# A two-block transformer on one core: expert weights in 16 KB runs, buffers of two units, three modulation steps moved, overflow loads issued by GpSimd

## Chip, cores and metric

One core of a Trainium2 chip runs the whole program in one launch. The metric is the device time of one execution in microseconds, the median of several. All inputs lie in the chip's memory in layouts that the host has prepared; preparing them is not timed. Engines: PE multiplies, PEld loads its weights, DVE, ACT and POOL (GpSimd) do the vector work, SP only issues transfers, and 16 DMA engines carry them.

## What is computed

256 tokens of width 1024, all in f32. Block 1 is attention with 8 heads, a layer norm, a mixture of 32 experts of which each token uses four, and another layer norm. Block 2 is two layers of attention (16 heads) and a gated feed-forward net, each modulated by vectors that come from `c` through `w_mod`.

```
t = moba_attention(h, w_in, w_out, rel_bias)
h = layer_norm(ALPHA * h + t)
top_logit, top_e = top_k(h @ w_router + b_router, 4); gate = softmax(top_logit)
# for each expert e and the tokens that chose it:
a = xs @ w_gu[e] + b_gu[e];  g, u = split(a)           # w_gu[e]: 1024 x 2048
g = min(g, 7);  u = clip(u, -7, 7)
y = (g * sigmoid(1.702 * g) * (u + 1)) @ w_down[e] + b_down[e]   # w_down[e]: 1024 x 1024
h = layer_norm(ALPHA * h + sum over the 4 of gate * y)
for i in range(2):                                      # block 2
    mod = silu(c) @ w_mod[i] + b_mod[i]                 # 1024 x 6144: six shifts, scales, gates
    x = x + gt_a * rmsnorm(attention(modulate(rmsnorm(x), sh_a, sc_a)) @ w_o[i])
    h = modulate(rmsnorm(x), sh_f, sc_f)
    x = x + gt_f * rmsnorm((silu(conv(h @ w_gate)) * (h @ w_up)) @ w_down[i])
```

## The kernel before

**The weight stream.** Every weight matrix comes as a row of 547 units of 1 MB, each a tile of 128 partitions x 2048 f32 and each used once. `Stream` (from L63) holds their order. `pump` (L85) issues the next unit on SP (L100) as soon as one of the open pools has a free buffer; `take` (L111) hands the next unit to the code that uses it, counts the one before as free and pumps. The pools are m (11 buffers, from the start), x (2 more, opened in the attention) and y (5 more, opened when the attention's space is given back, for units up to expert 20, closed at expert 24). A call of `take` fixes only the order; on the chip SP waits, instruction by instruction, until the engine that reads the old content is done. SP's transfers use eight semaphores in turn, so eight are under way at most.

**Order of the units** (`make_stream`, L204): queries, keys and values of attention 1, with four units of `w_mod` between them; four of `w_out`; then for each expert e eight gate-up units and four down units of expert e-1; the last expert's four down units; four units of `w_mod`; the weights of block 2. A gate-up unit is 128 rows of `w_gu[e]`, 8 KB a partition in one run. A down unit is 256 rows of `w_dn[e]`, two runs of 4 KB a partition.

**The expert loop** (`moe`, L798). PE multiplies the 64 token slots of an expert with the units in f32: `gate_up` (L698; bias L706, matmuls L715, eight a unit in the trace, since an f32 matmul shows twice) and `down` (L772, matmuls L783). Between the units it transposes and gathers for the neighbouring experts (L692, L740, L750, L763, L765) and adds the previous expert's rows (L795). In expert 24 comes `overflow` (L908): a branch (L916) on the largest count of tokens of an expert. Its body handles counts over 64, with loads of its own on SP; it is not entered with these inputs, but its branch stands on every engine.

**Modulation.** `fill` (L244) does n modulation steps: one unit of `w_mod`, four matmuls with `c` (L241). Four steps stand in the attention loop (`MOD_A`), four at the start of block 2 (`MOD_PRE`).

**Routing** (`norm1`, from L582): for each half of 128 tokens the residual sums (L597), `bn_stats` (L674), scaling (L599), transposes (L606), logits (L560, copy L622, sum L624), choice (L627 to L635). PE runs warm-up matmuls (L161) in its gaps; `WARM` gives their numbers.

Of the kernel before, what the change touches and what calls it, by code (L numbers as in the profile page):

```python
# [18 lines left out]
P = 128  # L19
# [10 lines left out]
NWB = 11  # L30
NXB = 2
NYB = 5
TOE = 16
OVER = 24
MOD_A = (1,1,1,1,0,0,0,0,0,0)
MOD_A_LAST = max(i for i in range(10) if MOD_A[i])
DVE_MOD = {(0, 1): 0, (1, 0): 0}
WARM = (8, 20, 4, 4, 4)
# [3 lines left out]
MOD_PRE = ((4, 0), (6, 0))  # L42
# [20 lines left out]
class Stream:  # L63
    def __init__(self, nc, srcs):
        self.nc = nc
        self.srcs = srcs
        self.pools = {}
        self.order = []
        self.tiles = {}
        self.where = {}  # L70
        self.issued = 0
        self.taken = 0
        self.limit = {}
        self.after = {}
        self.hold = len(srcs)
# [8 lines left out]

    def pump(self):  # L85
        while self.issued < self.hold:
# [7 lines left out]
            t = self.pools[key][0].tile([P, UNIT], F32, name=f"wu_{key}", tag=f"wu_{key}")  # L94
            src = self.srcs[i]
            if isinstance(src, list):
                for c0, c1, part in src:
                    self.nc.sync.dma_start(t[:, c0:c1], part)
            else:
                self.nc.sync.dma_start(t, src)  # L100
            for f in self.after.pop(i, ()):
                f()
            self.tiles[i] = t
            self.where[i] = key
            self.issued += 1
# [5 lines left out]
    def take(self):  # L111
        i = self.taken
        if i > 0:
            self.pools[self.where[i - 1]][1] += 1
            self.tiles.pop(i - 1)
            self.pump()
        self.taken += 1
        return self.tiles[i]


class Kernel:
# [79 lines left out]
    def make_stream(self):  # L201
# [10 lines left out]
        for i in range(10):  # L212
            u.append(ap["w_qk"][i] if i < 8 else outs[i - 8])
            m(MOD_A[i])
        u.extend(outs[2:])
        gu = lambda e: u.extend(ap["w_gu"][e, k * P:(k + 1) * P, :] for k in range(NK))
        dn = lambda e: u.extend(ap["w_dn"][e, k * 256:(k + 1) * 256, :].rearrange("(j p) n -> p j n", p=P) for k in range(4))
# [6 lines left out]
        dn(NE - 1)  # L224
        self.moe_end = len(u)
        self.stream_l2(u, m)
        self.st = Stream(self.nc, u)

# [15 lines left out]
    def fill(self, n, pool, pause=False):  # L244
# [3 lines left out]
        for i in range(n):  # L248
# [3 lines left out]
            if self.mps is None:  # L252
                self.mps = self.bank("acc", "modps")
# [101 lines left out]
    def attention1(self, a, a2):  # L355
# [44 lines left out]
        self.st.after = {2: [early], 3: [router], 5: [toeplitz_write], 6: [toeplitz_read], 8: [load_x], 10: [later]}  # L400
        self.st.hold = 5
# [92 lines left out]
        for i in range(10):  # L494
# [13 lines left out]
            self.fill(MOD_A[i], a2, i == MOD_A_LAST)()  # L508
# [12 lines left out]
        self.flush_mod()  # L521
        self.pause_mod()()
# [59 lines left out]
    def norm1(self):  # L582
# [12 lines left out]
        def rows(t):  # L595
            for h in range(2):
                nc.vector.scalar_tensor_tensor(x[:, t, hs[h]], x[:, t, hs[h]], ALPHA, self.ybank[h][t], op0=ALU.mult, op1=ALU.add)  # L597
            self.layer_stats([x[:, t, hs[0]], x[:, t, hs[1]]], t, mv, rs)
# [19 lines left out]
        def logits(t):  # L618
# [3 lines left out]
            nc.scalar.copy(part, ps[:, 0:P])  # L622
            lgs[t] = self.bank("acc")
# [18 lines left out]
        self.warm(WARM[4], "sc", self.cst.bitcast(BF16))  # L642
# [4 lines left out]
        self.warm(WARM[2], "sc", self.cst.bitcast(BF16))  # L647
        choose(1)

# [10 lines left out]
        self.warm(WARM[3], "sc", self.cst.bitcast(BF16))  # L660
# [7 lines left out]
        nc.vector.tensor_copy(self.cnt, cm)  # L668

    def layer_stats(self, halves, t, mv, rs):  # L670
        nc = self.nc
        bs = self.mk.tile([P, 2, 6], F32, name="bs", tag=f"bs{t}")
        for h in range(2):
            nc.vector.bn_stats(bs[:, h, :], halves[h])  # L674
# [214 lines left out]
    def norm2(self, banks, lnp):  # L889
# [5 lines left out]
        for t in range(2):  # L895
            self.layer_stats(banks[t], t, mv, rs)
# [10 lines left out]
    def overflow(self, banks):  # L907
# [8 lines left out]
        with tc.If(rv > CAP):  # L916
            with tc.For_i(0, NE, 1) as e:
# [10 lines left out]
                def gu_unit(k):  # L928
                    t = unit()
                    nc.sync.dma_start(t, ap["w_gu"][bass.ds(e, 1), k * P:(k + 1) * P, :].rearrange("o p n -> (o p) n"))  # L930
                    return t

                def dn_unit(k):
                    t = unit()
                    nc.sync.dma_start(t.rearrange("p (j n) -> p j n", j=2),
                                      ap["w_dn"][bass.ds(e, 1), k * 256:(k + 1) * 256, :].rearrange("o (j p) n -> p (o j) n", p=P))
# [547 lines left out]
```

## Time and profile before

| what | value |
|---|---|
| runs | 1736.28, 1736.58, 1737.66 us; median 1736.58 |
| profiled execution, its own time | 1736.98 us |
| its span | 1735.3 us |
| PE busy | 1672.9 us, 96% of the span |
| DVE, ACT, POOL busy | 739.8, 484.4, 82.3 us |
| moved by the DMA engines | 584.92 MB, mean 337 GB/s |
| first and last gate-up or down matmul | 135.84 us and 1072.8 us |

The span runs from the first instruction to the last; the execution's time lies 1.7 us above it. A busy share is an average over attention 1 with the routing (to 136 us), the MoE (to 1073 us) and block 2. PE's share counts a matmul as busy until its modelled end. A DMA share over 1 means that packets of one engine overlap.

### The profile page before, as it was taken

What the parts mean: (1) busy time and instruction counts of PE and PEld (TensorE: products, weight loads), DVE (VectorE), ACT (ScalarE), POOL (GpSimd) and SP (SyncE); (2) the same over time, 40 slices, a digit from 0 to 9 for tenths busy, and PEclk for the clock granted to TensorE, in tenths of its full rate; (3) what the DMA queues carried; (4) which work ended last, traced back from release to release, by engine and by line L of the source; (5) the groups of instructions that cost most, each with busy time, mean ns of one, the idle gap of its engine ahead of it and who ended that gap; (6) DMA issues with size and microseconds to landing.
All of it is one profiled execution on the core that took longest, in us unless ns stands there. A gap on an engine that the chain in (4) does not pass through costs nothing.

```text
span 1735.3 us, 23418 instructions
## 1 busy us (share of the span) xinstructions
PE 1672.9 (96%) x9690; PEld 975.5 (56%) x9690; DVE 739.8 (43%) x1196; ACT 484.4 (28%) x806; POOL 82.3 (5%) x113
## 2 busy tenths in 40 slices
PE   9999999999999999999899998999999999999998
PEld 6873333333333332333233322787999868879997
DVE  4662121221222112121121213896666867766654
ACT  4531000000001000000000001555655356565543
POOL 0000000000000020000000000031000003200000
PEclk9999999999999999999999999999999999999999
DMA  9969999999999999999989999974855986585520
GB/s 304 413 250 383 419 416 417 417 416 417 416 418 416 417 417 417 417 416 418 412 358 418 415 418 416 420 275 159 365 205 171 353 324 193 162 323 200 194 73 25
DMA packets 105655, 584.92 MB, mean 337 GB/s; under 512 B 11856, under 2 KB 13352, under 8 KB 54984
## 3 DMA queue, kind: packets, MB, share of 16 engines
q1 hardware_dynamic: 103736, 577.96, 83.5%
q0 software_dynamic: 1808, 5.41, 1.3%
q8 instruction: 78, 1.28, 0.3%
q14 instruction: 33, 0.27, 0.0%
HBM read 582.05 MB, written 1.28 MB: 336 GB/s over the span
## 4 chain that ended last, share of the span: by engine, by line
PE 36%; DMA 9%; DVE 3%; issue 1%; ACT 1%; POOL 0%; DVEq 0%; POOLq 0%; ACTq 0%; SPq 0%
PE ps_mm L145 6%; PE ps_mm L146 5%; PE ps_mm L147 5%; DMA wu_m<-w_dn 5%; DMA wu_m<-w_gu 3%; PE ps_sc L145 3%; PE ps_sc L146 3%; PE ps_sc L147 3%; PE ps_mm L715 1%; PE modps L241 1%; PE ps_acc L145 1%; DMA wu_x<-w_gu 1%; PE ps_acc L147 1%; PE ps_acc L146 1%; PE ps_tr L783 1%
## 5 line engine op out<-in xcount | busy, mean ns | idle before, releaser
L715 PE MATMUL ps_mm<-wu_m,xg 128*64 128x512 f32 x1400 | 329.1, 602 | 4.8 <-DMA wu_m<-w_gu 4.1
L140 DVE TENSOR_TENSOR wL<-wu_m,wH 128x1024 fp32r<-128x1024 f32 x226 | 267.3, 1225 | 142.5 <-ACT wH L139 142.5
L139 ACT CAST wH<-wu_m 128x1024 fp32r<-128x1024 f32 x226 | 225.9, 1049 | 104.2 <-PE ps_mm L146 66.2
L715 PEld LDWEIGHTS ps_mm<-wu_m,xg 128*64 128x64 f32 x1400 | 92.8, 137 | 198.0 <-issue 168.5
L783 PE MATMUL ps_tr<-wu_m,aT 128*64 128x512 f32 x752 | 174.7, 597 | 18.1 <-DMA wu_m<-w_dn 16.8
L145 PE MATMUL ps_mm<-hH,wH 128*128 128x256 f32 x608 | 174.9, 288 | 0.0
L147 PE MATMUL ps_mm<-hL,wH 128*128 128x256 f32 x608 | 172.0, 283 | 0.2 <-DVE hL L1060 0.2
L146 PE MATMUL ps_mm<-hH,wL 128*128 128x256 f32 x608 | 171.9, 283 | 0.0
L783 PEld LDWEIGHTS ps_tr<-wu_m,aT 128*64 128x64 f32 x752 | 50.6, 136 | 137.2 <-issue 82.6
L145 PEld LDWEIGHTS ps_mm<-hH,wH 128*128 128x128 f32 x608 | 116.4, 191 | 7.8 <-issue 6.5
L147 PEld LDWEIGHTS ps_mm<-hL,wH 128*128 128x128 f32 x608 | 116.5, 192 | 0.4 <-DVE hL L1060 0.4
L146 PEld LDWEIGHTS ps_mm<-hH,wL 128*128 128x128 f32 x608 | 116.5, 192 | 0.0
L787 DVE SCALAR_TENSOR_TENSOR yL<-ps_tr,gs,yH 128x512 fp32r<-128x512 f32 x32 | 24.0, 751 | 214.3 <-ACT yH L786 214.3
L695 ACT COPY gs<-ps_tr 128x512 f32<-128x512 f32 x32 | 18.8, 586 | 339.1 <-PE ps_tr L692 339.1
L769 DVE COPY gs<-ps_tr 128x1 f32<-128x1 f32 x32 | 5.1, 158 | 236.9 <-ACT s L767 236.9
L146 PE MATMUL ps_sc<-hH,wL 128*128 128x256 f32 x352 | 99.7, 283 | 0.0
L145 PE MATMUL ps_sc<-hH,wH 128*128 128x256 f32 x352 | 99.6, 283 | 0.0
L147 PE MATMUL ps_sc<-hL,wH 128*128 128x256 f32 x352 | 99.6, 283 | 0.0
L786 ACT ACTIVATE yH<-ps_tr,gs 128x512 fp32r<-128x512 f32 x32 | 22.0, 687 | 242.8 <-PE ps_tr L783 242.8
L715 PE MATMUL ps_mm<-wu_y,xg 128*64 128x512 f32 x368 | 85.9, 599 | 0.0
L730 ACT ACTIVATE sg<-g 128x512 f32<-128x512 f32 x32 | 20.2, 631 | 212.8 <-DVE g L729 212.8
L742 DVE COPY aT<-ps_tr 128x512 f32<-128x512 f32 x32 | 22.1, 691 | 132.6 <-PE ps_tr L740 132.6
(346 smaller groups left out, 2525.7 us busy)
## 6 DMA issues: line engine op xcount, KB each, us to landing
wu_m<-w_gu SPq DMA_DIRECT2D x175, 1024.0 KB, 19.9
wu_m<-w_dn SPq DMA_DIRECT2D x94, 1024.0 KB, 20.0
wu_m<-w_mod SPq DMA_DIRECT2D x48, 1024.0 KB, 6.7
wu_y<-w_gu SPq DMA_DIRECT2D x46, 1024.0 KB, 19.8
wu_m<-w_fg_u SPq DMA_DIRECT2D x44, 1024.0 KB, 8.2
wu_x<-w_gu SPq DMA_DIRECT2D x35, 1024.0 KB, 19.9
wu_m<-w_qk SPq DMA_DIRECT2D x24, 1024.0 KB, 13.1
wu_m<-w_fd SPq DMA_DIRECT2D x22, 1024.0 KB, 5.0
```

The costliest lines, as they stand in the source:

```text
L139: nc.scalar.copy(h[:, sl], src[:, sl])
L140: nc.vector.tensor_tensor(lo[:, sl], src[:, sl], h[:, sl].bitcast(F32), op=ALU.subtract)
L145: mm(out, lh, rh, start=start, stop=False)
L146: mm(out, ll, rh, start=False, stop=False)
L147: mm(out, lh, rl, start=False, stop=stop)
L695: nc.scalar.copy(gs, g)
L715: mm(ab[i][64 * h:64 * h + 64, :], self.chunk(xg, k), u[:, c:c + 512], start=False, stop=k == NK - 1, tile_position=(0, 64 * h))
L730: nc.scalar.activation(sg, g, AF.Sigmoid, scale=1.702)
L742: nc.vector.tensor_copy(aT, tp)
L783: nc.tensor.matmul(o[64 * h:64 * h + 64, :], lhs, u[:, c:c + 512], start=f == 0, stop=f == NK - 1, tile_position=(0, 64 * h))
L786: nc.scalar.activation(yH, o, AF.Copy, scale=gate)
L787: nc.vector.scalar_tensor_tensor(yL, o, gate, yH.bitcast(F32), op0=ALU.mult, op1=ALU.subtract)
```

## The change

1. **Pairs.** Units are taken in pairs. A buffer is a tile [128, 2, 2048] and comes free when both units are used. The pools are 5, 1 and 3 pairs (18 units as before). Where the next two units are a `Pair`, one transfer of 2 MB loads both; elsewhere two transfers of 1 MB as before.
2. **Layouts.** The host lays `w_gu` and `w_dn` out in pairs, so that a partition's share of a pair is one run of 16 KB. All experts' gate-up units and the down units of experts 0 to 30 are `Pair`s; the last expert's four down units are single transfers with 8 KB runs. `w_fd` of block 2 gets 8 KB runs for 4 KB.
3. **Modulation.** The four steps leave the attention loop; three stand in the routing, where eight warm-up matmuls leave, and at the start of block 2 there are five instead of four, behind 16 warm-up matmuls instead of 20.
4. **`layer_stats`** computes half a row's residual and its statistics in turn, where both residuals came first.
5. **Overflow** loads are issued on GpSimd's queue instead of SP's.
6. At the start the stream holds after six units instead of five, and the bias table's store and load come after units 6 and 7.

```diff
-NWB = 11
-NXB = 2
-NYB = 5
+NWB = 5
+NXB = 1
+NYB = 3
-MOD_A = (1,1,1,1,0,0,0,0,0,0)
-MOD_A_LAST = max(i for i in range(10) if MOD_A[i])
+MOD_A = 3
-WARM = (8, 20, 4, 4, 4)
+WARM = (8, 16, 4)
-MOD_PRE = ((4, 0), (6, 0))
+MOD_PRE = ((5, 0), (6, 0))
...
+    def load(self, t, src):
+        if isinstance(src, list):
+            for c0, c1, part in src:
+                self.nc.sync.dma_start(t[:, c0:c1], part)
+        else:
+            self.nc.sync.dma_start(t, src)
     def pump(self):
         while self.issued < self.hold:
             for key in self.order:
...
                 return
             i = self.issued
             self.pools[key][1] -= 1
-            t = self.pools[key][0].tile([P, UNIT], F32, name=f"wu_{key}", tag=f"wu_{key}")
-            src = self.srcs[i]
-            if isinstance(src, list):
-                for c0, c1, part in src:
-                    self.nc.sync.dma_start(t[:, c0:c1], part)
-            else:
-                self.nc.sync.dma_start(t, src)
-            for f in self.after.pop(i, ()):
-                f()
-            self.tiles[i] = t
+            t = self.pools[key][0].tile([P, 2, UNIT], F32, name=f"wu_{key}", tag=f"wu_{key}")
+            n = min(2, len(self.srcs) - i)
+            if isinstance(self.srcs[i], Pair):
+                self.nc.sync.dma_start(t, self.srcs[i].ap)
+            for j in range(i, i + n):
+                if not isinstance(self.srcs[i], Pair):
+                    self.load(t[:, j - i, :], self.srcs[j])
+                for f in self.after.pop(j, ()):
+                    f()
+                self.tiles[j] = t[:, j - i, :]
             self.where[i] = key
-            self.issued += 1
+            self.issued += n
     def resume(self):
         self.hold = len(self.srcs)
...
     def take(self):
         i = self.taken
         if i > 0:
-            self.pools[self.where[i - 1]][1] += 1
             self.tiles.pop(i - 1)
-            self.pump()
+            if i % 2 == 0:
+                self.pools[self.where[i - 2]][1] += 1
+                self.pump()
         self.taken += 1
         return self.tiles[i]
+class Pair:
+    def __init__(self, ap):
+        self.ap = ap
...
-        for i in range(10):
-            u.append(ap["w_qk"][i] if i < 8 else outs[i - 8])
-            m(MOD_A[i])
-        u.extend(outs[2:])
-        gu = lambda e: u.extend(ap["w_gu"][e, k * P:(k + 1) * P, :] for k in range(NK))
-        dn = lambda e: u.extend(ap["w_dn"][e, k * 256:(k + 1) * 256, :].rearrange("(j p) n -> p j n", p=P) for k in range(4))
+        u.extend(ap["w_qk"][i] for i in range(8))
+        u.extend(outs)
+        m(MOD_A)
+        def pairs(w):
+            for d in range(w.shape[0]):
+                u.extend([Pair(w[d].rearrange("p (j n) -> p j n", j=2)), None])
+        gu = lambda e: pairs(ap["w_gu"][e])
+        dn = lambda e: pairs(ap["w_dn"][e])
         for e in range(NE):
             gu(e)
             if e > 0:
                 dn(e - 1)
             if e == OVER - 4:
                 self.y_end = len(u)
-        dn(NE - 1)
+        u.extend(self.dn_part(ap["w_dn"][NE - 1], k) for k in range(4))
         self.moe_end = len(u)
         self.stream_l2(u, m)
         self.st = Stream(self.nc, u)
+    def dn_part(self, w, k):
+        return w[k // 2, :, (k % 2) * UNIT:(k % 2) * UNIT + UNIT]
...
-        self.st.after = {2: [early], 3: [router], 5: [toeplitz_write], 6: [toeplitz_read], 8: [load_x], 10: [later]}
-        self.st.hold = 5
+        self.st.after = {2: [early], 3: [router], 6: [toeplitz_write], 7: [toeplitz_read], 8: [load_x], 10: [later]}
+        self.st.hold = 6
...
-            self.fill(MOD_A[i], a2, i == MOD_A_LAST)()
...
         def rows(t):
-            for h in range(2):
+            def half(h):
                 nc.vector.scalar_tensor_tensor(x[:, t, hs[h]], x[:, t, hs[h]], ALPHA, self.ybank[h][t], op0=ALU.mult, op1=ALU.add)
-            self.layer_stats([x[:, t, hs[0]], x[:, t, hs[1]]], t, mv, rs)
+                return x[:, t, hs[h]]
+            self.layer_stats(half, t, mv, rs)
...
             nc.scalar.copy(part, ps[:, 0:P])
+            self.fill(1, a2, False, "sc")
             lgs[t] = self.bank("acc")
             mm(lgs[t][:, 0:NE], part, self.eyes, start=True, stop=True)
...
         logits(0)
-        self.warm(WARM[4], "sc", self.cst.bitcast(BF16))
         turn(1)
         turned(1)
         choose(0)
         logits(1)
-        self.warm(WARM[2], "sc", self.cst.bitcast(BF16))
         choose(1)
+        partial = self.fill(MOD_A - 2, a2, True, "sc")
...
+        partial()
...
-            nc.vector.bn_stats(bs[:, h, :], halves[h])
+            nc.vector.bn_stats(bs[:, h, :], half(h))
...
-                    nc.sync.dma_start(t, ap["w_gu"][bass.ds(e, 1), k * P:(k + 1) * P, :].rearrange("o p n -> (o p) n"))
+                    nc.gpsimd.dma_start(t, ap["w_gu"][bass.ds(e, 1), k // 2, :, (k % 2) * UNIT:(k % 2) * UNIT + UNIT].rearrange("o p n -> (o p) n"))
...
-                    nc.sync.dma_start(t.rearrange("p (j n) -> p j n", j=2),
-                                      ap["w_dn"][bass.ds(e, 1), k * 256:(k + 1) * 256, :].rearrange("o (j p) n -> p (o j) n", p=P))
+                    nc.gpsimd.dma_start(t, ap["w_dn"][bass.ds(e, 1), k // 2, :, (k % 2) * UNIT:(k % 2) * UNIT + UNIT].rearrange("o p n -> (o p) n"))
...
-    A["w_gu"] = asc(f("moe_w_gate_up")[0])
+    A["w_gu"] = asc(f("moe_w_gate_up")[0].reshape(NE, 4, 2, P, UNIT).transpose(0, 1, 3, 2, 4).reshape(NE, 4, P, 2 * UNIT))
-    A["w_dn"] = asc(f("moe_w_down")[0])
+    A["w_dn"] = asc(f("moe_w_down")[0].reshape(NE, 2, 4, P, D).transpose(0, 1, 3, 2, 4).reshape(NE, 2, P, 2 * UNIT))
...
-    A["w_fd"] = asc(f("w_ffn_down_2"))
+    A["w_fd"] = asc(f("w_ffn_down_2").reshape(2, NF // 2, 2, P, D).transpose(0, 1, 3, 2, 4).reshape(2, NF // 2, P, UNIT))
```

How the change stands in the programs, first on SP around the overflow branch (a row is the line, the instruction, and its target, source and shape; `x4` is four alike). Before:

```order
L100 DMA wu_m<-w_dn 128x2x1024 x4
L915 TENSOR_LOAD cnt
L916 COMPARE_AND_BRANCH
L917 COMPARE_AND_BRANCH
L917 UNCONDITIONAL_BRANCH x2
L1480 BRANCH_PREFETCH_HINT
L917 ISA
L930 DMA wu_o<-w_gu 128x2048
...
L916 UNCONDITIONAL_BRANCH
L100 DMA wu_x<-w_gu 128x2048 x2
L100 DMA wu_m<-w_gu 128x2048 x6
```

On SP around the branch now:

```order
L105 DMA wu_m<-w_dn 128x4096
L938 TENSOR_LOAD cnt
L939 COMPARE_AND_BRANCH
L940 COMPARE_AND_BRANCH
L940 UNCONDITIONAL_BRANCH x2
L1503 BRANCH_PREFETCH_HINT
L940 REGISTER_ALU
L940 COMPARE_AND_BRANCH
L940 UNCONDITIONAL_BRANCH
L939 UNCONDITIONAL_BRANCH
L105 DMA wu_m<-w_dn 128x4096
L105 DMA wu_m<-w_gu 128x4096 x3
```

The loads of the branch's body (`wu_o`) have left SP; they stand on POOL. The weights around the branch are transfers of two units.

SP from the end of attention 1 into the first experts, where the last free buffers of the MoE are filled. On SP before:

```order
L100 DMA wu_m<-w_out 128x2048 x4
L100 DMA wu_m<-w_gu 128x2048 x7
L100 DMA wu_x<-w_gu 128x2048 x2
L100 DMA wu_m<-w_gu 128x2048 x3
L100 DMA wu_y<-w_gu 128x2048 x4
L100 DMA wu_y<-w_dn 128x2x1024
L100 DMA wu_m<-w_dn 128x2x1024 x3
```

On SP at the same place now:

```order
L91 DMA wu_m<-w_out 128x2048 x4
L91 DMA wu_m<-w_mod 128x2048 x3
L105 DMA wu_m<-w_gu 128x4096
L105 DMA wu_x<-w_gu 128x4096
L105 DMA wu_m<-w_gu 128x4096 x2
L105 DMA wu_y<-w_gu 128x4096 x3
L105 DMA wu_m<-w_gu 128x4096
L105 DMA wu_m<-w_dn 128x4096 x2
```

Three units of `w_mod` stand between `w_out` and the experts; twenty units lie ahead of the first expert instead of twenty-one. The y pool now takes the fifth to seventh pair of the MoE.

PE in the routing, second half of the tokens (strips of the logits, their sum; `modps` is a modulation step, `h_87` holds the constants that count the choices). On PE before:

```order
L606 MATMUL ps_tr<-cst,x 128x128 x8
L560 MATMUL ps_acc<-xhT_1216,wr 32x128 x2
...
L624 MATMUL ps_acc<-cst,part 128x32
L161 LDWEIGHTS cst
L161 MATMUL warm<-cst 128x512
...
L652 LDWEIGHTS h_87
L652 MATMUL ps_acc<-Mb,h_87 128x32
```

On PE at the same place now:

```order
L628 MATMUL ps_tr<-cst,x 128x128 x8
L580 MATMUL ps_acc<-xhT_1165,wr 32x128 x2
...
L264 MATMUL modps<-wu_m,cact 32x512 x4
L647 MATMUL ps_acc<-cst,part 128x32
L264 MATMUL modps<-wu_m,cact 32x512 x4
L674 LDWEIGHTS h_87
L674 MATMUL ps_acc<-Mb,h_87 128x32
```

One step stands ahead of the sum of the logits and one behind it, where four warm-up matmuls stood.

## Rows read from the trace of the kernel before

**Rows 1.** The page: PE and moved bytes in 40 slices of the span

```profile
PE   9999999999999999999899998999999999999998
...
GB/s 304 413 250 383 419 416 417 417 416 417 416 418 416 417 417 417 417 416 418 412 358 418 415 418 416 420 275 159 365 205 171 353 324 193 162 323 200 194 73 25
```

**Rows 2.** Timeline of PE, experts 20 to 22: start, length, line [idle<-releaser]

```profile
696.02 3.65 PE L715 MATMUL ps_mm<-wu_m,xg 128*64 128x512 f32 x16
...
722.20 1.94 PE L783 MATMUL ps_tr<-wu_y,aT 128*64 128x512 f32 x8 [0.61 <-DMA wu_y<-w_dn]
...
726.14 3.65 PE L715 MATMUL ps_mm<-wu_m,xg 128*64 128x512 f32 x16
...
756.26 3.65 PE L715 MATMUL ps_mm<-wu_m,xg 128*64 128x512 f32 x16
```

**Rows 3.** Timeline of PE, first gate-up matmuls of two buffered experts

```profile
206.81 3.65 PE L715 MATMUL ps_mm<-wu_y,xg 128*64 128x512 f32 x16
...
233.75 1.94 PE L715 MATMUL ps_mm<-wu_x,xg 128*64 128x512 f32 x8
```

**Rows 4.** Windows: length; PE, PEld, DVE, ACT, POOL busy; clock, DMA share, GB/s

```profile
711.60:716.00 4.40, 4.40 (x23) 1.52 (x24) 2.75 (x4) 0.63 (x1) 0.00 (x0) 1.00 1.03 411
722.60:735.60 13.00, 13.00 (x62) 3.96 (x60) 1.83 (x4) 0.69 (x1) 0.00 (x0) 1.00 1.01 422
```

**Rows 5.** The DMA view of the same two stretches: packets by size

```profile
DMA packets 465, 1.81 MB, mean 411 GB/s; under 512 B 23, under 2 KB 23, under 8 KB 465
...
DMA packets 749, 5.48 MB, mean 422 GB/s; under 512 B 80, under 2 KB 80, under 8 KB 80
```

**Rows 6.** Timeline of SP around the overflow branch

```profile
846.63 10.39 SPq L100 DMA_DIRECT2D wu_m<-w_dn  x4
875.47 0.83 SPq L100 DMA_DIRECT2D wu_x<-w_gu  x2
```

**Rows 7.** The branch's line by engine: ns min/median/max, first to last start

```profile
L916 SPq EVENT_SEMAPHORE  x8: 17/17/17, 872.4 to 875.3; - x8
...
L916 PEldq COMPARE_BRANCH  x1: 7114/7114/7114, 844.9 to 844.9; - x1
```

**Rows 8.** Windows, columns as in rows 4

```profile
114.00:140.00 26.00, 22.95 (x141) 12.66 (x141) 14.07 (x47) 3.50 (x11) 2.04 (x3) 1.00 0.57 217
140.00:840.00 700.00, 680.95 (x3306) 234.60 (x3304) 151.14 (x270) 59.39 (x103) 15.04 (x6) 1.00 1.02 417
840.00:900.00 60.00, 53.61 (x262) 19.54 (x260) 8.74 (x17) 5.10 (x9) 0.00 (x0) 0.94 0.91 371
866.00:878.00 12.00, 12.00 (x64) 4.71 (x62) 4.31 (x7) 1.18 (x3) 0.00 (x0) 1.00 0.52 193
```

**Rows 9.** Timeline of SP at the start of the MoE

```profile
121.29 1.68 SPq L100 DMA_DIRECT2D wu_y<-w_gu  x3
```

**Rows 10.** Timeline of PE, a modulation step in attention 1

```profile
36.61 1.06 PE L241 MATMUL modps<-wu_m,cact 128*32 128x512 f32 x8
```

**Rows 11.** Timeline of the routing, DVE and PE

```profile
121.90 1.28 DVE L674 BATCH_NORM_STATS2 bs<-x 128x6 f32<-128x512 f32 x2
...
128.11 0.41 PE L624 MATMUL ps_acc<-cst,part 128*128 128x32 f32 x2 [0.65 <-ACT part L622]
```

**Rows 12.** Timeline of the start of block 2

```profile
1070.48 0.14 PEld L783 LDWEIGHTS ps_tr<-wu_m,aT 128*64 128x64 f32 x2 [0.31 <-DMA wu_m<-w_dn]
...
1081.61 3.64 PE L241 MATMUL modps<-wu_m,cact 128*32 128x512 f32 x32 [1.87 <-DVE x L902]
...
1085.64 1.98 ACT L139 CAST wH<-wu_m 128x1024 fp32r<-128x1024 f32 x2
...
1085.80 1.07 PE L1039 MATMUL ps_tr<-cst,xs 128*128 128x128 f32 x8 [0.55 <-DVE xs L1026]
```

**Rows 13.** The page: the queue that fetches instructions (packets, MB, share)

```profile
q8 instruction: 78, 1.28, 0.3%
```

**Rows 14.** The page: issues of one kind, us from issue to landing

```profile
wu_m<-w_fd SPq DMA_DIRECT2D x22, 1024.0 KB, 5.0
```

More of the change, by code (lines that the diff above doesn't have):

```diff
@@ L242, in mod_step, with fill @@
                                   start=start, stop=stop, tile_position=(0, 32 * j))
-    def fill(self, n, pool, pause=False):
+    def fill(self, n, pool, pause=False, tag="acc"):
         nc = self.nc
@@ L252, in fill @@
             if self.mps is None:
-                self.mps = self.bank("acc", "modps")
+                self.mps = self.bank(tag, "modps")
                 self.mod_first = k
@@ L520, in attention1 @@
             self.w_cur = nxt
-        self.flush_mod()
-        self.pause_mod()()
         w2 = (self.w_cur, self.split(self.st.take(), 2))
@@ L659, in norm1 @@
         nc.vector.tensor_scalar(self.posm, self.posm, -1.0, None, op0=ALU.add)
-        self.warm(WARM[3], "sc", self.cst.bitcast(BF16))
+        self.warm(WARM[2], "sc", self.cst.bitcast(BF16))
         self.oh0 = self.one_hot(lambda t: self.posm[:, t, 0:1])
@@ L668, in norm1, with layer_stats @@
         nc.vector.tensor_copy(self.cnt, cm)
-    def layer_stats(self, halves, t, mv, rs):
+        partial()
+    def layer_stats(self, half, t, mv, rs):
         nc = self.nc
@@ L895, in norm2 @@
         for t in range(2):
-            self.layer_stats(banks[t], t, mv, rs)
+            self.layer_stats(lambda h: banks[t][h], t, mv, rs)
         nm = m1.tile([P, 2], F32, name="nm2")
@@ L979, in stream_l2 @@
             for j in range(NF // 2):
-                u.append(ap["w_fd"][l, j * 256:(j + 1) * 256, :].rearrange("(j p) n -> p j n", p=P))
+                u.append(ap["w_fd"][l, j])
                 if l == 0 and 0 < j <= NK:
```

## Prediction, made before the changed kernel ran

> **What bounds the kernel now.** I read the page first, from top to bottom. The slices show PE busy nine tenths everywhere, which alone would make PE the bound; but from the fifth slice to the twenty-fifth the DMA engines are full as well, at 412 to 419 GB/s but for one slice of 358 [rows 1]. To see which of the two sets the pace, I go to the timeline of PE in the expert loop. In the steady part each of the last down units starts after an idle time that a transfer of `w_dn` ended, and the first gate-up matmul of an expert comes every 30.12 us: 696.02, 726.14, 756.26 [rows 2]. Earlier, where units lie ready in the buffers, the same expert takes 26.94 us, from 206.81 to 233.75 [rows 3]. So PE could give an expert in about 27 us and the transfers give one in 30.12: the MoE is DMA-bound by 3.2 us an expert, and until a transfer gets 10% faster, what it gains is gained in full.
>
> Next I ask what a unit costs the DMA engines. Every unit is 1 MB, but gate-up units move in runs of 8 KB and down units in runs of 4 KB. A stretch with down packets alone moves 411 GB/s and one with gate-up packets alone 422 GB/s, both with a DMA share over 1 [rows 4]. That is 1.0486 MB / 411 = 2.551 us and 1.0486 / 422 = 2.485 us a unit; eight and four of them make 19.88 + 10.20 = 30.08 us, the 30.12 of the timeline within 0.04. The 0.066 us between the units is what eight more packets on each of 16 engines cost: 8.3 ns a packet. The same stretches by packet, with the shares of 1.03 and 1.01: 1.03 x 16 x 4.4 us over 465 - 23 = 442 packets is 164 ns for 4 KB, 1.01 x 16 x 13 over 749 - 80 = 669 is 314 ns for 8 KB [rows 4, 5]; twice 164 less 314 leaves 14 ns. A packet thus has a fixed part of 8 to 14 ns.
>
> Last, the one place where the DMA engines stand still inside the MoE. SP issues four `w_dn` units from 846.63 on and nothing more until 875.47 [rows 6]. Between lie its branch at the overflow and, on the branch's line, eight semaphore steps from 872.4 to 875.3 [rows 7]: with the body not entered, SP first waits until its own eight transfers in flight have landed. The stretch 866 to 878 has a DMA share of 0.52, and 840 to 900 as a whole 371 GB/s, where 140 to 840 has 1.02 and 417 [rows 8].
>
> **The change part by part.**
>
> *Runs of 16 KB.* A pair is one transfer with one 16 KB run in each partition, so eight packets an engine instead of sixteen (gate-up) or thirty-two (down). An expert's 128 packets an engine become 48. One 16 KB run of weights is nowhere in the trace, so the cost is extrapolated: two gate-up units less eight packets of 8.3 ns are 4.970 - 0.066 = 4.90 us; six pairs make 29.4 us, against 30.08 to 30.12. I take 0.68 us an expert. PE's 26.94 us stays below, so nothing else becomes the bound. The first expert's four gate-up pairs load while attention still runs; the 186 pairs behind them are 31 experts' worth: 31 x 0.68 = **-21.1 us**. Bounds: if the engine cuts the run into packets of 8 KB, only down units gain, 4 x 0.066 x 31 = -8.2; with 14 ns a packet, 80 x 14 ns x 31 = -34.7. Below these stand the rivals "no gain" and "dearer". I take the first value since it goes by landed bytes, not by packet times, which overlap (a share of 1.01 to 1.03).
>
> The Trainium skill, page "DMA: Bandwidth & Descriptors", section "Why small descriptors are slow (HBM only)", gives each packet a fixed overhead of about 3 cycles on top of one for each 32 bytes. By it 4, 8 and 16 KB would be 131, 259 and 515 cycles, so 8 KB over 4 KB would bring 1.2%; the rows show 2.7% (411 to 422 GB/s) [rows 4], so the fixed part here looks more than twice that of the Trainium skill. What its smaller part would give is among the rivals.
>
> *Overflow transfers on GpSimd.* SP's body in the branch no longer holds DMAs, so on the skipped path it has no counts to make up and nothing to wait for. The hole goes: 12 us at a share of 0.52 instead of 1.02 is 5.9 us, and 60 us at 371 instead of 417 GB/s is 6.6. I take **-5.8 us** (-5 to -6.6; less, if the engines lose something there in any case, as while PE stands). The same duty moves to GpSimd, which has only the long-landed `b_dn` to look at, and no work there until the MoE is over; it costs nothing. PE's own 7.1 us at its branch [rows 7] stay; buffers of 12 units (the third pool is closed by then) hold 29 us of transfers, so SP goes on filling behind it.
>
> *Pairs as buffers.* 18 units before and after, but a buffer is free only when both units are used, half a pair (one unit, 2.5 us) later on average, of a queue over 40 us deep. In the steady state that is hidden. It shows at the start of the MoE. Before, the DMA engines have a share of 0.57 from 114 to 140 us [rows 8], because every buffer is full; the y buffers open only at 121.29 [rows 9], and by 140 the 18 first MoE units are there. Afterwards the first expert fills four pairs, and the last `w_out` and the modulation units hold the rest of what is open, so until about 114 only 8 MoE units are loaded; then three y pairs and, as `w_out` and the modulations are used, further pairs keep the queue full. From 114 to 140 that is 26 us less 2.5 of first latency (a unit in a near-empty queue lands after 5.0 us [rows 14], 2.5 of them its own) = 23.5 us, 9.5 units: 17.5 instead of 18, with the queue running instead of just starting. I put **+1.5 us** on it (0 to +4).
>
> *Three modulation steps into the routing.* One step takes PE 1.06 us [rows 10]; four leave attention, so it ends some 4.2 us earlier. In the routing three come in for eight warm-up matmuls: the first takes the place of four; the second stands ahead of the logits matmul of the second half, which waited 0.65 us for ACT's copy [rows 11], so 1.06 - 0.65 = 0.4 us are added; the third takes the place of the other four; the interleaved `bn_stats` gives back one of two, 0.64 us [rows 11]. All of it starts the MoE some 4.5 us earlier on PE, but the MoE ends with its last transfer, so this is worth only what it does to the transfers, which the item on pairs holds.
>
> *Five modulation steps at the handover.* One more unit lies between the last down unit and `w_v`: 2.5 us later. The modulations start at 1081.61, after DVE [rows 12], not after a transfer. ACT starts to split `w_v` at 1085.64 [rows 12]; the last down unit had landed by 1070.48 [rows 12], and five units with 8 KB runs, 2.485 us each, later, at 1082.9, `w_v` was there, 2.7 us ahead; so 0.2 us are left. PE's fifth step costs 0.9 us, of which 0.55 was idle behind the fourth [rows 12]. I take **+0.3 us** (0 to +3.4, the end where the step's 0.9 and a whole unit of 2.5 both fall on the path). The four warm-ups less ahead of the steps lengthen PE's idle time before 1081.61 from 1.87 us [rows 12] and delay nothing that waits.
>
> *The wait for a pair.* The first unit of a pair can be used only when both have landed, and PE's matmuls stand in order behind that wait. In the steady part 3.65 us of gate-up matmuls [rows 2] then follow in the 4.90 until the next pair, so nothing falls behind, and the last four down units stay single, so the end is not put off: nothing.
>
> *Block 2* moves 25 to 365 GB/s (27th slice on [rows 1]), less than the engines give, so runs of 8 KB for `w_fd` and pairs as buffers change nothing there.
>
> **Sum.** -21.1 - 5.8 + 1.5 + 0.3 = -25.1, of which the last three are -4.0. The profiled execution took 1736.98, its span 1735.3; 1736.98 - 25.1 = 1711.9. The median of the runs is 0.4 lower, so **1711.5**.
>
> **The rivals.**
>
> *The run pays less.* Packets of at most 8 KB: -8.2 in place of -21.1, so 1736.6 - 8.2 - 4.0 = **1724.5**. For it: no weight packet over 8 KB has been seen. Against it: the instruction queue's 78 packets are 1.28 MB, 16 KB each [rows 13], so the engines do carry that size whole. 9%.
>
> *The fixed part of a packet is half as large*, and the other half of 411 against 422 comes from how down rows lie in memory: 80 x 4.1 ns x 31 = 10.2 us, so 1736.6 - 10.2 - 4.0 = **1722.5**. Against it: 14 ns from the packets' own times [rows 5]. 5%. The Trainium skill's 3 cycles, in the section named above, are such a part: by them 0.6% of gate-up and 1.7% of down time would go, an estimate of 9 us in all.
>
> *It pays more*, the 14 ns in full: 1736.6 - 34.7 - 4.0 = **1698**; 6%.
>
> *It pays nothing*, because 420 GB/s is a limit of the memory and not of packets: only the other three terms are left, so **1732.6**, 0.23% below the median, which a measurement may as well call the same. Against it: 411 and 422 in neighbouring stretches with full engines. 5%.
>
> *Slower: a 16 KB packet is dearer than two of 8 KB.* The only ones in the trace take 0.3% of 16 x 1735.3 us over 78, 1.07 us each [rows 13], against 2 x 0.314. An expert would be 48 x 1.07 = 51 us, 21 more, and the kernel about 2390; the point from which this decides is 0.630 us a packet (30.25 / 48, the 4.0 us of the other terms spread over 31 experts), and at 0.66 us, 5% over two small ones, it is 31 x 1.56 = 48 us less the 4.0, about **1781**. For it: these are the only rows of that size. Against it: they are fetches of code, not of weights, few and on another queue, and from 4 to 8 KB the time less than doubles [rows 5]. 8%.
>
> *SP still waits at the branch* (the change doesn't do what it says): 1711.5 + 5.8 = **1717**. For it: the branch keeps a tail on every engine. Against: SP's part of the branch's body has no DMA any more. 4%.
>
> **How the numbers follow.** The forecast, 1706 to 1717 by its small terms and by 0.6 to 0.8 us an expert, has 63%; with the rivals at 1724.5, 1722.5 and 1717 the range **1702 to 1727** holds 81%; it leaves out 1698, "nothing" and "dearer". A measurement of this kernel can tell about 0.2%, 3.5 us, from no change. Faster: 63 + 9 + 5 + 6 + 4 = 87%; same 5%; slower 8%.
>
> **What would show it.** First gate-up matmuls of experts 20 to 23 29.4 us apart (29.9 in the weak case); about 428 GB/s in the stretches that now show 411 and 422; no gap of SP's issues near the branch and no slice under 410 GB/s there; the last down matmul some 24 us earlier; block 2 unchanged in length, with PE's first split matmul not waiting for `w_v` by over 0.5 us. The prediction is wrong if packets of 16 KB are cut or take over 0.630 us, or if PE waits in block 2 for transfers that pairs hold back.

## The result, and the profile of the changed kernel

The changed kernel took 1714.92 us (median; 1713.94 to 1716.45), the kernel before 1737.08 in the same rounds: a ratio of 0.9873, 95% interval 0.9861 to 0.9885, or 22 us less. The profiled execution took 1715.33 us with a span of 1713.7, 21.6 less than before.

The page of the changed kernel, span, slices and packets, answers to [rows 1]:

```profile
span 1713.7 us, 22958 instructions
...
PE   9999999999999999999899997999999999999998
...
GB/s 294 323 279 427 428 428 428 428 427 428 426 427 428 428 428 427 427 427 427 426 428 428 428 427 414 345 197 235 328 196 197 373 266 221 161 333 188 181 123 25
DMA packets 59090, 584.85 MB, mean 341 GB/s; under 512 B 8816, under 2 KB 10312, under 8 KB 13544
```

The MoE moves 427 GB/s for 417, and the slice of 358 is gone: in the slices the whole of it reads 426 to 428. The timeline of PE in experts 20 and 21 (start, length, line, idle before and its releaser) answers to [rows 2]; the expert period is 714.44 - 685.07 = 29.37 us:

```profile
685.07 3.65 PE L738 MATMUL ps_mm<-wu_x,xg 128*64 128x512 f32 x16
...
708.79 3.65 PE L806 MATMUL ps_tr<-wu_y,aT 128*64 128x512 f32 x16 [1.14 <-DMA wu_y<-w_dn]
...
714.44 3.65 PE L738 MATMUL ps_mm<-wu_m,xg 128*64 128x512 f32 x16
```

The branch by engine (the rows of line 939) answers to [rows 7]. SP has no semaphore steps any more; POOL has four, at 638.8, far from any work:

```profile
L939 POOLq EVENT_SEMAPHORE  x4: 17/43/43, 638.8 to 639.0; - x4
...
L939 SPq COMPARE_BRANCH  x1: 50/50/50, 827.2 to 827.2; - x1
```

SP's timeline there answers to [rows 6]; SP goes on issuing behind the branch:

```profile
826.29 5.10 SPq L105 DMA_DIRECT2D wu_m<-w_dn  x2
841.76 11.63 SPq L105 DMA_DIRECT2D wu_m<-w_gu  x3
```

The end of the MoE and the start of block 2 on PE answer to [rows 12]:

```profile
1035.02 3.65 PE L806 MATMUL ps_tr<-wu_m,aT 128*64 128x512 f32 x16 [1.18 <-DMA wu_m<-w_dn]
...
1042.15 7.09 PE L806 MATMUL ps_tr<-wu_m,aT 128*64 128x512 f32 x32
...
1058.08 5.89 PE L264 MATMUL modps<-wu_m,cact 128*32 128x512 f32 x40 [2.74 <-DVE x L925]
...
1069.10 0.50 PE L161 MATMUL ps_mm<-wH,hH 128*128 128x512 f32 x1 [1.20 <-ACT hH L1079]
```

The last down matmul ends at 1049.24, 23.5 us earlier than before. The landing of the last unit can be read from the trace's semaphore events: 1044.91, before 1070.44, so the transfers are 25.5 us earlier. The other 4 us were lost on the way to the end: 2.0 between the last landing and the last down matmul, 0.5 from there to the first matmul of block 2 (1069.10; before 1092.10, 19.3 us behind its last down matmul), and 1.4 in block 2.

### The profile page after: what moved, and what is told of

It is laid out like the page before. It is cut to its first block, busy times and chain, and to the rows that moved or that the text cites. A ratio compares the mean times of both kernels' runs of the same rounds, so it can differ in the third digit from the quotient of the medians.

```text
span 1713.7 us, 22958 instructions
## 1 busy us (share of the span) xinstructions
PE 1658.3 (97%) x9678; PEld 980.9 (57%) x9678; DVE 739.9 (43%) x1196; ACT 484.6 (28%) x806; POOL 77.8 (5%) x113
## 4 chain that ended last, share of the span: by engine, by line
PE 40%; DMA 6%; DVE 3%; issue 1%; ACT 1%; POOL 0%; DVEq 0%; POOLq 0%; ACTq 0%
DMA wu_m<-w_dn 6%; PE ps_mm L161 5%; PE ps_mm L163 5%; PE ps_mm L162 5%; PE ps_sc L161 3%; PE ps_sc L162 3%; PE ps_sc L163 3%; PE ps_mm L738 3%; PE ps_tr L806 2%; PE modps L264 2%; PE ps_acc L161 1%; PE ps_acc L163 1%; PE ps_acc L162 1%; DVE macc L318 1%; DVE wL L156 1%
## 5 line engine op out<-in xcount | busy, mean ns | idle before, releaser
L738 PE MATMUL ps_mm<-wu_m,xg 128*64 128x512 f32 x1200 | 279.1, 600 | 5.5 <-DMA wu_m<-w_gu 5.1
L806 PE MATMUL ps_tr<-wu_m,aT 128*64 128x512 f32 x800 | 179.7, 595 | 19.2 <-DMA wu_m<-w_dn 19.2
L738 PEld LDWEIGHTS ps_mm<-wu_m,xg 128*64 128x64 f32 x1200 | 79.7, 137 | 165.8 <-issue 143.8
L806 PEld LDWEIGHTS ps_tr<-wu_m,aT 128*64 128x64 f32 x800 | 57.0, 137 | 138.2 <-issue 101.2
L738 PE MATMUL ps_mm<-wu_y,xg 128*64 128x512 f32 x448 | 103.5, 598 | 1.1 <-DMA wu_y<-w_gu 1.1
L738 PE MATMUL ps_mm<-wu_x,xg 128*64 128x512 f32 x400 | 91.2, 598 | 0.0
L753 ACT ACTIVATE sg<-g 128x512 f32<-128x512 f32 x32 | 20.2, 630 | 212.4 <-DVE g L752 212.4
```

What stands on the lines that cost most here:

```text
L738: mm(ab[i][64 * h:64 * h + 64, :], self.chunk(xg, k), u[:, c:c + 512], start=False, stop=k == NK - 1, tile_position=(0, 64 * h))
L753: nc.scalar.activation(sg, g, AF.Sigmoid, scale=1.702)
L806: nc.tensor.matmul(o[64 * h:64 * h + 64, :], lhs, u[:, c:c + 512], start=f == 0, stop=f == NK - 1, tile_position=(0, 64 * h))
```

## The experiments

**Runs of 8 KB.** The pairs stay one transfer of 2 MB; only the layout differs (`w_dn`, left out here, is laid out alike).

```diff
-                u.extend([Pair(w[d].rearrange("p (j n) -> p j n", j=2)), None])
+                u.extend([Pair(w[d].rearrange("j p n -> p j n")), None])
...
-    A["w_gu"] = asc(f("moe_w_gate_up")[0].reshape(NE, 4, 2, P, UNIT).transpose(0, 1, 3, 2, 4).reshape(NE, 4, P, 2 * UNIT))
+    A["w_gu"] = asc(f("moe_w_gate_up")[0].reshape(NE, 4, 2, P, UNIT))
...
```

> The changed kernel with its pairs laid out so that a partition's 16 KB come in two runs of 8 KB; still one transfer of 2 MB a pair, same buffers and order. Theory (a packet has a fixed cost of 8.3 ns, read from 411 and 422 GB/s in the kernel before): an expert has 96 packets an engine for 48, 48 x 8.3 ns = 0.40 us an expert, 31 experts, +12.4 us on 1714.9, so 1727; expert period 29.8 us, 421 to 423 GB/s in the MoE. Rival one (half the fixed cost, 4.1 ns): +6, so 1721. The Trainium skill's 3 cycles a packet, an estimate: +5, so 1720. Rival two (the larger transfer, not the longer run, brought the gain): +0, 1715.

1728.45 us, 13.6 above the changed kernel's 1714.8 to 1714.9. **Runs of 4 KB**, with the layouts cut once more:

> The same with four runs of 4 KB a partition and pair. Theory: 192 packets for 48, 144 x 8.3 ns = 1.20 us an expert, +37 us, so 1752; period 30.6 us, 411 GB/s throughout. With 14 ns a packet: +62, so 1777. Rival one (4.1 ns): +18, so 1733. Rival two: 1715.

1756.29 us, 41.4 above. The windows from 250 to 800 us of the changed kernel and these two, in this order, and the first gate-up matmuls of two experts of the 8 KB kernel (columns as in [rows 4] and [rows 2]):

```profile
250.00:800.00 550.00, 531.59 (x2610) 187.29 (x2608) 117.05 (x210) 45.60 (x80) 15.03 (x6) 1.00 1.01 427
```

```profile
250.00:800.00 550.00, 527.89 (x2574) 185.91 (x2572) 113.75 (x206) 44.93 (x79) 15.01 (x6) 1.00 1.01 421
```

```profile
250.00:800.00 550.00, 508.24 (x2474) 177.70 (x2472) 110.90 (x199) 43.31 (x76) 14.97 (x6) 1.00 1.02 409
```

```profile
693.10 3.65 PE L738 MATMUL ps_mm<-wu_x,xg 128*64 128x512 f32 x16
...
722.92 3.65 PE L738 MATMUL ps_mm<-wu_m,xg 128*64 128x512 f32 x16
```

The reader is to see 427, 421 and 409 GB/s at the same share, and a period of 29.82 us for 29.37. An engine carries 48 packets more for each of 31 experts with runs of 8 KB and 144 more with 4 KB. Per packet: 13.6 us / (31 x 48) = 9.1 ns and 41.4 / (31 x 144) = 9.3 ns. Two steps of very different size give the same price, so the run's length is the cause, in packets; the size of the transfer is not (1715 was its forecast for both). By the Trainium skill's 3 cycles a packet ("DMA: Bandwidth & Descriptors", "Why small descriptors are slow (HBM only)") the 8 KB kernel was to take 1720, an estimate; the measurement decides, and the fixed part is over twice that.

**The overflow's loads alone**, both ways: back on SP in the changed kernel, and on GpSimd in the kernel before. Of the edit, the first load in the changed kernel (the second, of `w_dn`, is moved alike):

```diff
-                    nc.gpsimd.dma_start(t, ap["w_gu"][bass.ds(e, 1), ...
+                    nc.sync.dma_start(t, ap["w_gu"][bass.ds(e, 1), ...
...
```

> The changed kernel with the overflow branch's loads back on SP, nothing else. Theory: SP again waits at the skipped branch until its transfers have landed, the hole comes back: +5.8 us (5 to 6.6), so 1720.7, with one slice of the MoE near 365 GB/s and SP silent for some 20 to 30 us. Rival (the hole came from PE's pause at its own branch, or the stream makes it up later): 1715, within 1 us of the changed kernel.

> The kernel before with the overflow branch's loads issued on GpSimd, nothing else. Theory: -5.8 us (5 to 6.6) on 1737.1, so 1731.3, the slice of 358 GB/s gone. Rival (the hole has another cause): 1737.

1717.01 us (2.1 above the changed kernel, ratio to before 0.9885, interval 0.987 to 0.99) and 1734.01 (3.7 below the kernel before, ratio 0.998, interval 0.9971 to 0.9989, that is 1.9 to 5.0 us). The 5.8 of the forecast lies outside. Yet the bytes are as forecast: SP's timeline in the first kernel shows the wait (first fence), and its window of 60 us at the branch loses 60 x (427 - 386) / 427 = 5.8 us of transfers (second fence, columns as in [rows 4]); in the second kernel the same 60 us as in [rows 8] have no hole left (third fence).

```profile
825.77 26.15 SPq L105 DMA_DIRECT2D wu_m<-w_dn  x2
852.04 2.09 SPq L105 DMA_DIRECT2D wu_m<-w_gu  x3
```

```profile
820.00:880.00 60.00, 55.48 (x270) 20.31 (x268) 11.16 (x21) 5.73 (x10) 0.00 (x0) 0.94 0.92 386
```

```profile
840.00:900.00 60.00, 54.83 (x270) 20.05 (x268) 9.61 (x18) 5.09 (x9) 0.00 (x0) 0.97 1.02 416
```

So the theory of where the hole comes from stood, and its price fell. Two-microsecond windows of the kernel before show why (the last number but one is the DMA share):

```profile
866.00:868.00 2.00, 2.00 (x14) 1.00 (x12) 0.00 (x0) 0.22 (x2) 0.00 (x0) 1.00 0.91 363
868.00:870.00 2.00, 2.00 (x14) 0.98 (x16) 0.16 (x1) 0.32 (x1) 0.00 (x0) 1.00 0.67 270
870.00:872.00 2.00, 2.00 (x14) 0.74 (x12) 0.47 (x1) 0.00 (x0) 0.00 (x0) 1.00 0.57 223
872.00:874.00 2.00, 2.00 (x12) 0.62 (x10) 0.91 (x2) 0.00 (x0) 0.00 (x0) 1.00 0.30 117
874.00:876.00 2.00, 2.00 (x12) 0.72 (x10) 1.54 (x3) 0.63 (x1) 0.00 (x0) 1.00 0.02 6
876.00:878.00 2.00, 2.00 (x12) 0.66 (x10) 1.23 (x2) 0.00 (x0) 0.00 (x0) 1.00 0.65 176
```

The engines do not stop together; they run dry one after another over 8 us, and all stand for some 2. Every transfer leaves 16 reports (semaphore events) in the trace, as many as there are engines; I read each as one engine's, sent when its part of the unit is there. The first and the last report of some units:

```
kernel           issued   first    last     apart
before           846.63   859.94   867.38   7.43
before           854.90   867.57   874.90   7.33
before           875.47   879.77   880.44   0.68
before           879.24   897.18   899.21   2.03
changed          826.29   845.36   852.26   6.90
```

A unit has landed with its last report. Ahead of the hole the fastest engine is 7.4 us ahead of the slowest, and its idle time does not put that landing off; for the slowest, the hole is the 5.54 us between the landings at 874.90 and 880.44 less a unit's 2.49, that is 3.05.

**A second hole**, in the kernel before, was to test that price.

```diff
-            if e == OVER:
-                self.overflow(banks)
+            if e in (OVER, OVER + 2):
+                self.overflow(banks, e == OVER)
...
```

> The kernel before with a second skipped overflow branch, with loads on SP, two experts after the first; its body is never entered. Theory (a unit has landed when the slowest of the 16 engines has brought its part; ahead of the first hole the engines end a unit 7.4 us apart, behind it 0.7 to 2 us; only the slowest engine's idle time counts, about 3 us, the gap between the last landing of the drained queue and the next, less a unit's 2.5): the second hole costs 3 us as the first does, 1740.3, though it loses fewer bytes than the first (some 4 us of transfers for 6.6), since the faster engines no longer end early. Rival (the cost is the bytes lost, and the stream made up half of the first hole later): the second costs 6 us or, by its bytes, 4; with 6, 1743.

1741.28 us: ratio 1.0025, interval 1.0016 to 1.0035, 2.8 to 6.1 us more, which leaves neither 3 nor 6 out. Its two windows of 60 us:

```profile
840.00:900.00 60.00, 53.16 (x256) 19.20 (x252) 8.32 (x17) 5.10 (x9) 0.00 (x0) 0.91 0.90 365
900.00:960.00 60.00, 53.94 (x258) 18.23 (x254) 12.22 (x21) 4.76 (x8) 0.00 (x0) 0.97 0.96 389
```

The second hole loses 60 x (417 - 389) / 417 = 4.0 us of transfers for the first one's 7.5: fewer, as the theory said. Its gap, from the landing at 941.00 to 946.41, less 2.49, is 2.9 us, as the first one's. But by the landing at 952.64 the stream is 4.2 us later than the kernel before, since one engine fell 1.3 us back just behind the hole (reports 0.4 us apart, then 1.7). The first hole has such a step too (0.7, then 2.0): unit by unit, the kernel before lands 0.5 us behind the one with GpSimd's loads ahead of the hole, 3.6 behind it and 5.0 with the step.

In return the drained stream is spared later: between its landings at 977.17 and 983.43 the kernel with GpSimd's loads falls back by 1.2 us while its reports go from 6.7 to 8.0 us apart, and the kernel before, whose reports are 2.1 apart, does not; at the last unit 3.5 us are left. The changed kernel with SP's loads has a gap of 4.2 us (from 851.30 to 860.36, less a pair's 4.90), so its landings lose 4.2 us at the branch; 1.1 of them come back by the last unit. Of the 3.1 that are left the times of the runs show 2.1; in its trace the clock at the start of block 2 stayed up, in the changed kernel's it fell, which is worth 0.5 to 0.8 us (below). The gap thus gives what a hole costs on the spot, and not what is left of it at the end.

What the steps are can be read from the packets of the queue that fetches instructions. From 250 to 840 us of the kernel before this queue moves 21 packets of 16 KB, and at each of the 21 the reports shift as if one engine fell back, by 1.2 to 1.6 us, while the others keep their pace (a report does not say whose it is); seven packets of 8 KB go with smaller steps, and no other step is over 0.25 us. From 250 to 820 us of the changed kernel it is again 21 of 21. The steps behind the two holes have their packets at 896.29 and 947.35, and the one that spares the drained stream at 978.62. No run takes the fetches away, so this rests on the times alone.

**The last expert but one in single units**, **20 warm-up matmuls** at block 2, and both, beside the changed kernel itself:

```diff
+            if e == NE - 1:
+                u.extend(self.dn_part(ap["w_dn"][e - 1], k) for k in range(4))
-            if e > 0:
+            elif e > 0:
```

```diff
-WARM = (8, 16, 4)
+WARM = (8, 20, 4)
```

> The changed kernel again, beside its variants: 1714.9 (1714 to 1716.5). If block 2's extra wait of 1.5 us for GpSimd's small transfer comes and goes from run to run, this trace lacks it or has it elsewhere; if it belongs to the change, it is there again.

> The changed kernel with the four down units of the last expert but one single too. Theory: the MoE's end is late because PE starts the last two down steps only when a whole pair has landed, so that its last down matmul ends 4.3 us or so behind the last landing instead of 2.3; with single units PE starts each at its landing, the end comes 1.5 to 2 us earlier, less 0.1 us for the shorter runs: 1713.2. Rival (PE's tail is set by the activation of the last expert and what lies between, not by the pair): 1715.

> The changed kernel with 20 warm-up matmuls ahead of the modulation steps at the start of block 2, as before. Theory: PE idles 2.7 us there now and runs the five steps at a granted clock of 0.51 for the first 3 us, taking 5.89 us instead of 4.55; with 20 the idle time is 1.85 and the steps take 4.6, but only some of it is on the path (DVE waited 0.24 us for them): -0.3 us, so 1714.6, and the steps at a granted clock of 1. Rival (the clock falls because of something else): steps again 5.9 us, 1714.9.

> Both of the last two edits. Theory: 1712.9; the two do not meet, so the sum of the two. Rival: as the better of them alone.

1714.79, 1713.11, 1714.31 and 1712.96 us, ratios 0.9872, 0.9862, 0.9866 and 0.9858, each with an interval of some 0.0035: the times follow the theory, but the intervals overlap, and only with both edits do all runs (1712.30 to 1713.05) lie below those of the changed kernel beside them (1714.54 to 1716.06). So it is the traces that carry it. With single units eight matmuls stand behind PE's last wait for a transfer where sixteen stood, and the last down steps come 2.2 us earlier (timeline of PE); the last down matmul ends 2.6 us behind the last landing for 4.3:

```profile
1034.54 1.94 PE L808 MATMUL ps_tr<-wu_m,aT 128*64 128x512 f32 x8 [0.55 <-DMA wu_m<-w_dn]
...
1039.96 7.09 PE L808 MATMUL ps_tr<-wu_m,aT 128*64 128x512 f32 x32
```

With 20 warm-ups (its timeline of PE, its window of 3 us, and the same window of the changed kernel) the idle time is 1.87 us for 2.74, the granted clock 1.00 for 0.51, the upper for the lower of its two levels, and the five steps take 4.50 us for 5.89:

```profile
1057.83 4.50 PE L264 MATMUL modps<-wu_m,cact 128*32 128x512 f32 x40 [1.87 <-DVE x L925]
```

```profile
1058.00:1061.00 3.00, 3.00 (x32) 0.91 (x28) 2.42 (x4) 1.78 (x5) 0.91 (x2) 1.00 1.02 415
```

```profile
1058.00:1061.00 3.00, 2.92 (x16) 0.80 (x20) 2.48 (x5) 1.78 (x6) 0.92 (x2) 0.51 1.01 421
```

That the number of warm-ups decides is not shown by this. Seven traces have 16 warm-ups and an idle time of 2.73 or 2.74 us behind them. In three (the changed kernel, its repeat, the one with single units) the clock fell and the five steps took 5.89 to 6.2 us; in four (runs of 8 KB, of 4 KB, SP's loads, and the next experiment) it did not, and they took 4.50. With 20 it fell in none of six. The timeline of PE in the next experiment, with 16:

```profile
1057.16 4.50 PE L265 MATMUL modps<-wu_m,cact 128*32 128x512 f32 x40 [2.74 <-DVE x L926]
```

**The modulation steps back in attention 1:**

```diff
-        u.extend(ap["w_qk"][i] for i in range(8))
+        for i in range(8):
+            u.append(ap["w_qk"][i])
+            m(int(i < MOD_A))
...
+            self.fill(int(i < MOD_A), a2, i == MOD_A - 1)()
...
-            self.fill(1, a2, False, "sc")
...
+        self.warm(4, "sc", self.cst.bitcast(BF16))
...
```

> The changed kernel with its three early modulation steps back in the attention loop (behind the first three query-key units) and eight warm-up matmuls back in the routing; five steps at block 2 as in the changed kernel. Theory: three steps of 1.06 us push the end of attention 1 back by 3.2 us; the y pool opens 3.2 us later (116.2 for 113.0), the DMA engines, idle by then, start their full stretch that much later, and the MoE's last transfer and the end come up to 3.2 us later; pairs of m come free earlier, since no modulation unit holds one into the routing, but they are behind y in the row of the queue and give nothing back: 1718.0. Rival (the transfers are set by when PE frees m pairs in the MoE, and PE's start is not on the path): 1714.9, DMA share of 114 to 140 as high as in the changed kernel.

1713.69 us, ratio 0.9867 (0.9852 to 0.9883): no 3 us later, if anything 1 earlier. SP's timeline shows that the y pool did open later, at 116.51, but that by then five pairs of the MoE had gone out, the fifth at 98.28, where the changed kernel (second fence) has four ahead of y and `w_mod` in the buffers:

```profile
98.28 0.33 SPq L105 DMA_DIRECT2D wu_m<-w_gu  x1
116.51 3.79 SPq L105 DMA_DIRECT2D wu_y<-w_gu  x3
```

```profile
90.77 11.54 SPq L105 DMA_DIRECT2D wu_m<-w_gu  x2
112.95 3.83 SPq L105 DMA_DIRECT2D wu_y<-w_gu  x3
```

My theory had this pair behind y and fell. The 1 us is not from the start: the last unit lands at 1044.01, in two traces of the changed kernel at 1044.91 and 1044.04. From the last down matmul to the first matmul of block 2 the trace takes 19.3 us for their 19.9 and 20.2, with the clock at its upper level. All three edits together:

> The changed kernel with all three edits that the runs so far showed at or ahead of it: single down units for the last expert but one, 20 warm-up matmuls at block 2, the three early modulation steps back in the attention loop. Theory: the first two give 1.8 us as before; the third gives 0.6 us at the last transfer (m pairs come free while attention still runs, so a fifth pair of the MoE is loaded ahead of y's opening): 1712.3. Rival (the third is nothing but the spread of runs): 1713.0.

1713.69 us, ratio 0.9869: no better than the first two alone, so the third brings nothing that can be told. The best version is the one with single units and 20 warm-ups, at 1712.96 us, 1.8 below the changed kernel beside it by medians.

## Why the prediction was right, and where its terms were not

The time, 1714.9, lies 3.4 us above the 1711.5 forecast and well inside 1702 to 1727. What bounded the kernel was read rightly: the MoE gained all that its transfers gained, and PE's 96% did not stand in the way. The last landing moved by 25.5 us where the terms that act on it (-21.1, -5.8 and +1.5) gave 25.4. That the time came so near is in part luck: the terms below were off by 5.5 to 7.3 us one way and by 3 the other. Term by term:

| term | forecast | shown by the runs |
|---|---|---|
| runs of 16 KB | -21.1 | -22.8 (9.2 ns x 80 x 31) |
| hole at the branch | -5.8 | -3.7 in the kernel before; in the changed one -2.1 by the runs, -3.1 by the landings |
| pairs at the start | +1.5 | +0.2 (landing of the twentieth MoE unit, mean of six traces with the new start, 146.71 to 147.37, and of three with the old one, 146.43 to 147.07) |
| the wait for a pair | 0 | +2.0 |
| handover | +0.3 | +0.5 (0 to +0.2 where the clock did not fall) |
| block 2 | 0 | +1.2 to 1.4 |
| sum | -25.1 | -22.6 to -20.8 by the experiments, -22 measured |

*Runs.* Right in kind and nearly in size: 9.2 ns a packet for 8.3. The expert period was forecast at 29.4 and is 29.37.

*The hole.* The step that failed is the pricing by the mean share: "12 us at a share of 0.52 instead of 1.02 is 5.9 us". A mean over 16 engines counts the idle time of engines that were up to 7.4 us ahead, and the landing of a unit goes by the slowest, which lost 3.05 us. With the step behind it the hole did put the landings off by 4.5 us, near the forecast; but part of this came back later, which the prediction had not considered, and 3.7 us are left in the kernel before and 2.1 to 3.1 in the changed one.

*The wait for a pair* was called nothing, since PE's 3.65 us fit into 4.90. That holds in the steady part and not at the end. There PE starts the last pair of `w_dn` of expert 30 only at 1035.02, and from then on has 3.65 us of that pair, the transposes and the previous expert's rows with 1 us of waiting, and 7.09 of the last expert: 14.2 us against four units of 2.49. Each of the last four units has landed when PE comes to it; the matmuls run 7.09 us without a wait. The prediction kept the last four single and looked for the bound in the transfers only.

*Handover.* The term had its size, but not its cause. From the last down matmul to the first matmul of block 2 the three traces with the old handover take 19.3 us. With five steps and the clock at its upper level it is 19.3 to 19.5, so the fifth step costs 0 to 0.2 us. In the three traces where the clock fell (0.51 in the changed kernel) the steps cost PE 1.4 to 1.7 us more, of which 0.3 to 0.8 was on the path (19.9 to 20.2); the prediction had no such term. The sentence that four warm-ups less delay nothing that waits held where the clock stayed up. Why it fell in these three and not in the four others with 16 warm-ups stays open.

*Block 2* was called unchanged on the ground that it is below the DMA rate. From its first matmul to the end of the span block 2 takes 643.2 to 643.4 us in the three traces with single units (the kernel before, with GpSimd's loads, with two holes) and 644.1 to 644.8 in the ten with pairs. Near 1480 us a two-step transfer through memory on POOL's queue waits 2.82 us for its first half, before 1.36 (2.29 to 2.85 in the ten, 1.35 to 1.58 in the three), and DVE then waits for POOL. Timelines of SP, POOL and DVE in the changed kernel, then of POOL before:

```profile
1470.35 0.80 SPq L91 DMA_DIRECT2D wu_m<-w_mod  x2
...
1479.62 0.57 POOL L1099 DMA_DIRECT2D gg<-ggd  x1 [2.82 <-DMA ggd<-ggr]
...
1480.65 1.49 DVE L1238 SCALAR_TENSOR_TENSOR nl<-ps_sc,cumt,cm 128x128 f32<-128x128 f32 x4 [1.51 <-POOL cm L1201]
```

```profile
1501.28 0.57 POOL L1077 DMA_DIRECT2D gg<-ggd  x1 [1.36 <-DMA ggd<-ggr]
```

A pair frees two units at once, so SP issues two loads together (1470.35, x2) where it issued one at a time. That this is what POOL's transfer meets was argued from the timing and not tried apart.

The rivals: "packets of at most 8 KB" and "a fixed part half as large" fell with the period of 29.37 and the two kernels with shorter runs; "it pays more" fell with their 9.1 and 9.3 ns for its 14, and "it pays nothing" with 427 GB/s for 417; "dearer", whose only row was the fetches of code, fell too: 16 KB of weights took 4.9 us / 8 = 0.61 us a packet against those fetches' 1.07. "SP still waits" fell with SP's timeline.

## What to carry to other kernels

Where every engine of a stream is full, count packets: the gain of longer runs was the same 9 ns for each packet saved, from 4 to 8 and from 8 to 16 KB, and could be read beforehand from two stretches with different runs. The mean share of the DMA engines overstates a hole in a stream where the engines are apart (6.6, 4.0 and 5.8 us in the three holes here); the gap between landings gives the loss on the spot (3.05, 2.9, 4.2), and what is left at the end has to be measured (3.7, 4.7 and 2.1 by the medians of the runs). When units are joined, look at the two ends where the joint unit is not hidden, the last consumer behind the last landing and the light traffic of other queues that now meets two loads at once.

## What I had not expected of the hardware

The 16 DMA engines bring the parts of one transfer up to 8.5 us apart in a full stream (7.4 in the kernel before, 6.9 in the changed one, 0.7 right after a drained queue, by the reports in the traces), and the landings fall back in steps of 0.3 to 1.4 us as this spread grows. In the traces these steps come with the packets that fetch instructions: at each of the 21 of 16 KB from 250 to 840 us of the kernel before, one engine fell back by 1.2 to 1.6 us. So fetching the program takes time from the weight stream, and how much of it reaches the landings depends on whether the engine that it falls on is the slowest.

And the same idle time behind the same warm-up matmuls can leave the granted clock up or bring it down: with 16 of them and 2.73 or 2.74 us of waiting, the steps ahead of block 2 ran at the lower level in three traces (0.51 over 3 us in the changed kernel) and at the upper one in four. With 20, and 1.87 us of waiting, it did not fall in any of six.
